# The MLP of a one-layer decoder trunk: sum of squares moved into the up phase, its buffers opened ahead, the first two weight pairs interleaved, the last results of the down product in turn

## The chip, the cores and the metric

The kernel runs on one core of one Trainium2 chip. The metric is device time in microseconds (us) of one execution; the number given for a kernel is the median of its runs. The engines are named as in the profile: PE is TensorE (matmuls; PEld is its weight load), DVE is VectorE, ACT is ScalarE, POOL is GpSimd, SP is SyncE, which here only starts DMAs, in the order of its queue.

## The reference, cut to what matters

One layer, 1024 tokens, model width 1024. After a mixer with three branches and a cross-attention come the parts that matter here:

```
h += CrossAttn(RMSNorm(h), RMSNorm(mem))       # its last step is a product with w_xo
h += W_down( relu(RMSNorm(h) @ W_up)^2 )       # W_up 1024 x 4096, W_down 4096 x 1024

def rms_norm(x, g):
    y = x * rsqrt(mean(x * x) + EPS)
    return y * g
```

Everything is fp32. The kernel holds activations transposed, channels on partitions and tokens along the free dimension: `h` is eight tiles `ht[0]` to `ht[7]` of 128 x 1024. The norm's factor is one number per token, and because `relu(r*x)^2 = r^2 * relu(x)^2` for a positive `r`, it can be left out of the up product and multiplied into the result of the down product. So the sum of squares of `h` over channels is needed only by the end of the down product's first half.

## The kernel before, in words

**Split matmuls.** A fp32 product is made of three matmuls with rounded operands: an operand is split into a rounded high part (a cast on ACT) and the rest (a subtraction on DVE, or on POOL for weights), and high x high, high x low and low x high are added up. In an activation's split the parts are called `oh` and `ol`, in a weight's split `wh` and `wl`; in the up phase one tile holds both: `blk` for activations, `st` for weights.

**The stages at the change.** Three stages follow each other.

1. *The last `w_xo` products* (`project`, L1293 to L1298, and the loop at L1346). Eight products of 24 matmuls each, in the order `ht` 0, 4, 1, 5, 2, 6, 3, 7, from the operands `parts1` (four pairs in pool `opa`). After each, DVE adds the result to `ht` (L1298), SP stores it to the scratch `d_h`, DVE scales it to `v` (L1355), ACT squares it (L1358, L1361) and POOL adds the squares up in `h_acc` (L1362). From the `v` of two tiles (i and i + 4) come the operands of the up phase. That is a Strassen-Winograd product: seven block products take the place of eight, so of each pair of `v` seven blocks are made by `slice_of` (L1331): four quarters or sums of quarters. The names are `x11`, `x21`, `x22` for quarters and `t1` to `t4` for sums of them; `t1` is made at L1367, `t2` at L1371, `t3` at L1375 and `t4` at L1377, all on DVE. `slice_of` casts on ACT (L1336) and subtracts on DVE (L1337). The blocks go into 28 buffers that other work has finished with (`spare`): last among them the tiles `ht` themselves, whose stores must have landed, and pool `opd`.
2. *The up phase* (L1412). Sixteen pairs of `w_up` tiles. For each pair two loads (`ws`: one half in the phase's own pool `up`, one in `wstage`, which the `w_xo` weights use too), three sums on DVE (`s`, L1422 to L1424, and one more at L1429), and seven `stationary` tiles `st`: a cast on ACT (L1407) and a subtraction on POOL (L1408), under high priority. The `st` rotate through ten buffers: six in the pool `wsplit`, which the `w_xo` weights use too, four tagged `oh` in `opa`. Seven products of 12 matmuls follow, in a written order (6, 1, 5, 7, 2, 3, 4; for the first pair 1, 5, 6, 2, 3, 7, 4). Their results go to the four banks `ps_up`, and DVE adds them up (`u`, `r`), squares (L1442) and SP stores them to `d_r`. The bank of product 5 is read until product 7 is done. In the first pair the factor is worked out (`factor`): a column sum by PE, a square root, a diagonal matrix `f_dg` (L260) and its product with ones (`ps_bs`), which spreads the factor over partitions as `rb`.
3. *The down phase* (L1484). Two halves of 512 output channels. Each reads all 32 tiles back from `d_r`, splits each (`split`, ACT L1053 and DVE L1054, four buffers each for `oh` and `ol` in `opb`) and multiplies it with four columns of weights into eight banks: for each tile 24 matmuls. When the 32nd is done, DVE multiplies each bank by `rb` into a tile `o` of two buffers (L1521). In the first half POOL adds `h` (`hv`, read back from `d_h`; L1526) and the whole tile is stored; in the second DVE adds it (L1523) and each half tile is stored.

**What sets the order.** The Tile scheduler orders each engine's instructions by a model of their times, in program order of priority, and each pool's tiles rotate through its buffers. A pool opened after another is closed may lie over its memory; then its tiles wait for what was there. `after(n, f)` calls `f` after n further steps, where a step is called after every few matmuls. The pool `pre`, which holds `v`, `t` and the squares, is closed before the pool `up` opens.

Of the kernel before, what the change touches and what calls it, by code (L numbers as in the profile page):

```python
# [9 lines left out]
F32 = mybir.dt.float32  # L10
# [7 lines left out]
P = 128  # L18
D = 1024
# [36 lines left out]
def trunk_kernel(tc, w_io):  # L56
# [3 lines left out]
    with ctx:  # L60
# [1279 lines left out]
        acc = xr.tile([P, T], F32, tag="acc", name="h_acc3")  # L1340
        with tc.tile_pool(name="pre", bufs=2) as tp:

            rbx = opd.tile([P, T], F32, tag="sl", name="rbx")
            dg = tp.tile([P, T], F32, tag="sq", name="hx_dg", bufs=1)
            after(0, lambda: spread(xr, rx[0], T, "hx", rbx, dg))
            for kp in range(4):  # L1346
                if kp % 2 == 0:
                    slots = [wslot(w_io["w_xo"][1, kp // 2 + 2 * q]) for q in range(2)]
                vs = []
                for q in range(2):  # L1350
                    i = kp + 4 * q
                    project(parts1, slots[q], i // 2, kp % 2)
                    nc.sync.dma_start(d_h[i], ht[i])
                    v = tp.tile([P, T], F32, tag="v", name="v")
                    dve.scalar_tensor_tensor(v, ht[i], C("g_mlp", i), rbx, ALU.mult, ALU.mult)  # L1355
                    vs.append(v)
# [6 lines left out]
                    lo_, hi_ = v[:, :512], v[:, 512:]  # L1363
                    if q == 0:
                        slice_of("x11", lo_)
                        t1 = tp.tile([P, 512], F32, tag="t1", name="t1", bufs=1)
                        dve.tensor_sub(t1, hi_, lo_)  # L1367
                        slice_of("t1", t1)
                t2, t3 = (tp.tile([P, 512], F32, tag="t", name="t") for _ in range(2))
                b12, (b21, b22) = vs[0][:, 512:], (vs[1][:, :512], vs[1][:, 512:])  # L1370
                dve.tensor_sub(t2, b22, t1)  # L1371
                slice_of("t2", t2)
                slice_of("x21", b21)
                slice_of("x22", b22)
                dve.tensor_sub(t3, b22, b12)  # L1375
                slice_of("t3", t3)
                dve.tensor_sub(t2, b21, t2)  # L1377
                slice_of("t4", t2)

        f = []  # L1380

        def factor():

            r = token_rstd(xr, acc, T, 1.0 / D, EPS, "hm")
# [9 lines left out]
        with ExitStack() as sc:  # L1394
            mp = sc.enter_context(tc.tile_pool(name="up", bufs=1))
            after(8, factor)
# [14 lines left out]
            ORDER = (6, 1, 5, 7, 2, 3, 4)  # L1411
            for pr in range(16):  # L1412
                order = ORDER if pr else (1, 5, 6, 2, 3, 7, 4)
                with tc.high_priority():
                    ws = []
                    for q in range(2):
                        w = (wst if q else mp).tile([P, 1024], F32, tag="ws", name="ws", bufs=2)
                        nc.sync.dma_start(w, w_io["w_up"][pr * 2 + q])
                        ws.append(w)
# [21 lines left out]
                def square(o):  # L1441
                    dve.scalar_tensor_tensor(o, o, 0.0, o, ALU.max, ALU.mult)  # L1442
# [192 lines left out]
```

## Time and profile before

| | us |
|---|---|
| median of three runs | 2801.35 |
| lowest and highest | 2796.13, 2801.6 |
| profiled execution | 2799.92 |
| its span, first to last instruction | 2798.1 |

| engine | busy us | share of the span | instructions |
|---|---|---|---|
| PE | 2702.5 | 97% | 12704 |
| PEld | 2181.8 | 78% | 12704 |
| DVE | 1637.3 | 59% | 1858 |
| ACT | 1058.9 | 38% | 1780 |
| POOL | 937.4 | 34% | 460 |

The span runs from the first to the last instruction. All positions in time below are microseconds from its start. The mean granted clock of PE is 0.986 of full speed. The stages of the change lie at the end: the eight `w_xo` products end at 2090.5, the up phase runs from 2113.5 to 2434.7, the down phase from there on.

### The profile page before, as it was taken

How to read it: one execution, taken by the hardware profiler on the slowest of the kernel's cores; microseconds unless marked ns; L12 is line 12 of the kernel's file. 1: busy time of each engine (PE TensorE's matmuls, PEld its weight loads, DVE VectorE, ACT ScalarE, POOL GpSimd, SP SyncE). 2: the span in 40 equal slices, each digit the busy share in tenths (PEclk: the TensorE clock that was granted, in tenths of full speed). 3: DMA queues.
4: the chain of work that ended last, by engine and by line, in shares of the span. 5: the costliest groups of instructions: out<-in, count | busy, mean ns of one | idle time of the engine just before them, and what ended most of it. 6: DMA issues, size and time to landing. Idle time of an engine off the chain costs nothing.

```text
span 2798.1 us, 32362 instructions
## 1 busy us (share of the span) xinstructions
PE 2702.5 (97%) x12704; PEld 2181.8 (78%) x12704; DVE 1637.3 (59%) x1858; ACT 1058.9 (38%) x1780; POOL 937.4 (34%) x460
## 2 busy tenths in 40 slices
PE   8899999999999999999899999999977999999998
PEld 6688878887787878765588778898765888888787
DVE  7678878759777876634414674233386666532322
ACT  6523321213565564556511352245333222233221
POOL 4622222201626252434242522421134554422320
PEclk9999999999999999999999999999997999999999
DMA  6552332321333233542443323311112332454541
GB/s 228 180 144 94 101 115 83 115 105 39 114 113 120 99 127 99 171 140 85 163 162 131 126 93 97 98 54 33 44 68 83 113 113 106 180 188 143 195 131 66
DMA packets 111225, 325.98 MB, mean 117 GB/s; under 512 B 10961, under 2 KB 35937, under 8 KB 110689
## 3 DMA queue, kind: packets, MB, share of 16 engines
q1 hardware_dynamic: 111072, 323.92, 34.4%
q8 instruction: 100, 1.64, 0.2%
q14 instruction: 53, 0.43, 0.1%
HBM read 248.22 MB, written 78.80 MB: 117 GB/s over the span
## 4 chain that ended last, share of the span: by engine, by line
PE 79%; DVE 10%; issue 4%; POOL 2%; DMA 2%; ACT 2%; SPq 0%; DVEq 0%; ACTq 0%; POOLq 0%
PE ps_g L73 34%; PE ps_d L73 12%; PE ps_tm L73 12%; PE ps_up L73 10%; DVE tapy L334 3%; PE ps_yd L73 2%; DVE c4a L744 1%; POOL wl L158 1%; PE ps_lg L73 1%; PE ps_xl L73 1%; PE ps_xo L73 1%; PE ps_pt L77 1%; PE ps_yo L73 1%; PE ps_stt L73 1%; ACT lg L977 1%
## 5 line engine op out<-in xcount | busy, mean ns | idle before, releaser
L158 POOL TENSOR_TENSOR wl<-ws,wh 128x1024 fp32r<-128x1024 f32 x168 | 427.7, 2550 | 1053.2 <-ACT wh L157 993.0
L334 DVE SCALAR_TENSOR_TENSOR tapy<-hin,cst,tapy 128x1024 f32<-128x1024 f32 x240 | 387.7, 1616 | 31.0 <-ACT tapy L329 24.7
L73 PE MATMUL ps_g<-uh,wh 128*128 128x512 f32 x1008 | 330.5, 407 | 12.0 <-ACT uh L353 12.0
L157 ACT CAST wh<-ws 128x1024 fp32r<-128x1024 f32 x168 | 176.2, 1050 | 422.8 <-PE ps_g L73 263.3
L73 PE MATMUL ps_up<-blk,st 128*128 128x512 f32 x1344 | 311.7, 394 | 24.5 <-ACT st L1407 23.0
L73 PE MATMUL ps_g<-ul,wh 128*128 128x512 f32 x1008 | 324.4, 396 | 0.3 <-DVE ul L354 0.3
L73 PEld LDWEIGHTS ps_up<-blk,st 128*128 128x128 f32 x1344 | 255.8, 191 | 80.1 <-ACT st L1407 23.4
L73 PE MATMUL ps_g<-uh,wl 128*128 128x512 f32 x1008 | 315.8, 392 | 1.3 <-POOL wl L158 1.3
L73 PE MATMUL ps_g<-oh,wh 128*128 128x512 f32 x768 | 247.5, 404 | 10.1 <-DVE ht L1298 6.0
L73 PE MATMUL ps_g<-ol,wh 128*128 128x512 f32 x768 | 239.4, 393 | 2.5 <-DVE ol L1054 2.4
L73 PE MATMUL ps_g<-oh,wl 128*128 128x512 f32 x768 | 238.1, 391 | 0.0
L1054 DVE TENSOR_TENSOR ol<-r_in,oh 128x1024 fp32r<-128x1024 f32 x64 | 94.4, 1476 | 234.0 <-ACT oh L1053 231.9
L73 PEld LDWEIGHTS ps_g<-ul,wh 128*128 128x128 f32 x1008 | 190.1, 189 | 50.0 <-issue 9.3
L73 PEld LDWEIGHTS ps_g<-uh,wl 128*128 128x128 f32 x1008 | 189.8, 188 | 43.2 <-POOL wl L158 2.7
L73 PEld LDWEIGHTS ps_g<-uh,wh 128*128 128x128 f32 x1008 | 178.9, 190 | 40.3 <-ACT uh L353 12.0
L73 PE MATMUL ps_d<-oh,wh 128*128 128x512 f32 x512 | 199.9, 390 | 4.4 <-DVE o L1521 4.4
L73 PE MATMUL ps_d<-ol,wh 128*128 128x512 f32 x512 | 199.7, 390 | 0.0
L73 PE MATMUL ps_d<-oh,wl 128*128 128x512 f32 x512 | 199.6, 390 | 0.0
L73 PEld LDWEIGHTS ps_g<-oh,wh 128*128 128x128 f32 x768 | 144.0, 190 | 47.0 <-issue 8.1
L73 PE MATMUL ps_tm<-wh,uh 128*128 128x512 f32 x448 | 175.7, 392 | 0.3 <-DVE zth L590 0.3
L73 PE MATMUL ps_tm<-wh,ul 128*128 128x512 f32 x448 | 174.5, 390 | 0.0
L73 PE MATMUL ps_tm<-wl,uh 128*128 128x512 f32 x448 | 174.3, 389 | 0.0
(380 smaller groups left out, 4676.1 us busy)
## 6 DMA issues: line engine op xcount, KB each, us to landing
ws<-w_ch SPq DMA_DIRECT2D x64, 512.0 KB, 3.4
r_in<-d_r SPq DMA_DIRECT2D x64, 512.0 KB, 3.7
csb<-d_cs SPq DMA_DIRECT2D x32, 512.0 KB, 3.9
gth<-d_th SPq DMA_DIRECT2D x32, 512.0 KB, 4.3
ws<-w_up SPq DMA_DIRECT2D x32, 512.0 KB, 3.2
d_r<-r SPq DMA_DIRECT2D x32, 512.0 KB, 2.6
ws<-w_down SPq DMA_DIRECT2D x32, 512.0 KB, 3.4
d_th<-gate_th SPq DMA_DIRECT2D x21, 512.0 KB, 5.1
```

Of the source, the lines that this page charges most:

```text
L73: ins = nc.tensor.matmul(*a, **k)
L77: ins = nc.tensor.transpose(*a, **k)
L157: act.copy(wh, st)
L158: pool.tensor_sub(wl, st, wh.bitcast(F32))
L334: dve.scalar_tensor_tensor(y, hin[:, j:j + T], w(j), y, ALU.mult, ALU.add)
L744: dve.scalar_tensor_tensor(a[:, s:], v[:, :T - s], C("c4_w", ct * 4 + 3 - s), a[:, s:], ALU.mult, ALU.add)
L977: act.activation(lg[:, i, k0:], lg[:, i, k0:], AF.Exp, bias=nm[:, i:i + 1], accum_out=rs[:, i:i + 1],)
L1054: dve.tensor_sub(b, src, a.bitcast(F32))
```

## The change

- `h`'s squares are no longer made in the first stage. During up pairs 2 to 9, before the first product of each, one tile of `h` is read back from `d_h` into an `ol` buffer of `opa`, squared in place on ACT and added up on POOL. `factor` is called at pair 11, not in the first pair.
- The pool `up` is opened ahead of the `w_xo` loop, and `pre` is gone: `v` and the first diagonal live in `opd`, `t1`, `t2` and `t3` in buffers of `up`. `spare` gives `opd`'s tiles later and the `ht` tiles earlier.
- Pairs 0 and 1 form one group: products 1 and 5 of pair 0, then 1 and 5 of pair 1, then 6, 2, 3, 7, 4 of pair 0 and of pair 1. All fourteen `st` of the group are asked for ahead of its products.
- In the last block of four tiles of a down half, the order is turned: all four tiles are split, and then each of the eight banks gets its remaining 12 matmuls in one go and is taken at once: multiplied, `hv` added on DVE, stored by half tiles, in both halves. `o` uses the eight `ht` buffers.

```diff
-            for pool_, tags, n in ((opc, ("oh", "ol"), 4), (opb, ("oh", "ol"), 4), (opd, ("sl",), 3)):
+            for pool_, tags, n in ((opc, ("oh", "ol"), 4), (opb, ("oh", "ol"), 4), (opd, ("sl",), 1)):
...
-            yield opd, "sl"
+            for _ in range(3):
+                yield opd, "sl"
...
-        acc = xr.tile([P, T], F32, tag="acc", name="h_acc3")
-        with tc.tile_pool(name="pre", bufs=2) as tp:
...
+        with ExitStack() as sc:
+            mp = sc.enter_context(tc.tile_pool(name="up", bufs=1))
...
-            dg = tp.tile([P, T], F32, tag="sq", name="hx_dg", bufs=1)
+            dg = opd.tile([P, T], F32, tag="sl", name="hx_dg")
...
-                    v = tp.tile([P, T], F32, tag="v", name="v")
+                    v = opd.tile([P, T], F32, tag="sl", name="v")
...
-                    if i == 0:
-                        act.activation(acc, ht[i], AF.Square)
-                    else:
-                        sq = tp.tile([P, T], F32, tag="sq", name="sq", bufs=1)
-                        act.activation(sq, ht[i], AF.Square)
-                        pool.tensor_add(acc, acc, sq)
...
-                        t1 = tp.tile([P, 512], F32, tag="t1", name="t1", bufs=1)
+                        t1 = mp.tile([P, 512], F32, tag="p1", name="t1", bufs=2)
...
-                t2, t3 = (tp.tile([P, 512], F32, tag="t", name="t") for _ in range(2))
+                t2 = mp.tile([P, 512], F32, tag="u2", name="t2")
+                t3 = mp.tile([P, 512], F32, tag="u5", name="t3")
...
-            after(8, factor)
...
+            def squares_of(i):
+
+                if i == 0:
+                    sums.append(xr.tile([P, T], F32, tag="acc", name="h_acc3"))
+                hq = opa.tile([P, T], F32, tag="ol", name="h_sq3")
+                nc.sync.dma_start(hq, d_h[i])
+                if i == 0:
+                    act.activation(sums[0], hq, AF.Square)
+                else:
+                    act.activation(hq, hq, AF.Square)
+                    pool.tensor_add(sums[0], sums[0], hq)
...
+            ORDER = (6, 1, 5, 7, 2, 3, 4)
+            groups = [[(0, 1), (0, 5), (1, 1), (1, 5)] + [(pr, j) for pr in range(2) for j in (6, 2, 3, 7, 4)]]
+            groups += [[(pr, j) for j in ORDER] for pr in range(2, 16)]
+            for group in groups:
+                pairs = {}
+                with tc.high_priority():
+                    for pr, j in group:
+                        if pr not in pairs:
+                            pairs[pr] = Pair(pr)
+                        pairs[pr].weights(j)
+                for pr, j in group:
+                    if j == ORDER[0] and 2 <= pr < 10:
+                        squares_of(pr - 2)
+                    elif j == ORDER[0] and pr == 11:
+                        after(0, factor)
+                    pairs[pr].product(j)
...
+                    if blk < 7:
+                        for k in range(4):
+                            operand(blk * 4 + k)
+                            for q in range(4):
+                                for h in range(2):
+                                    product(k, q, h)
+                                step()
+                        continue
+
+                    for k in range(4):
+                        operand(28 + k)
+                    for q in range(4):
+                        i = hf * 4 + q
+                        o = hp.tile([P, T], F32, tag=f"ht{i}", name="o")
+                        for h in range(2):
+                            sl = slice(h * 512, h * 512 + 512)
+                            for k in range(4):
+                                product(k, q, h)
                             step()
...
+                            dve.tensor_mul(o[:, sl], outs[q][h], f[0][:, sl])
+                            dve.tensor_add(o[:, sl], o[:, sl], hs[q][:, sl])
+                            nc.sync.dma_start(w_io["outT"][i][:, sl], o[:, sl])
```

The class `Pair` (new) holds the loads, sums, `st`, products and results of one pair as the loop before did, each made when it is first asked for; `operand(n)` reads tile n of `d_r` and splits it, `product(k, q, h)` is its three matmuls into one bank.

## Rows read from the trace of the kernel before

**Rows 1.** Table by stage: microseconds, busy time (instructions) of five engines, PE's clock, DMA.
```profile
2042.70:2058.50 15.80, 15.80 (x72) 13.07 (x71) 14.74 (x14) 6.63 (x9) 4.58 (x2) 1.00 0.16 66
2058.50:2090.50 32.00, 26.01 (x99) 20.00 (x97) 31.77 (x30) 13.32 (x20) 12.59 (x6) 0.89 0.23 91
2090.50:2113.50 23.00, 0.01 (x2) 0.01 (x1) 19.02 (x20) 7.72 (x13) 8.25 (x4) 0.55 0.22 80
2113.50:2145.00 31.50, 26.38 (x93) 19.59 (x93) 22.85 (x29) 9.97 (x17) 20.83 (x14) 0.77 0.25 84
2145.00:2434.70 289.70, 289.70 (x1274) 239.68 (x1273) 183.94 (x218) 75.23 (x119) 140.03 (x100) 1.00 0.31 114
2611.40:2618.80 7.40, 3.04 (x7) 1.82 (x6) 3.46 (x5) 1.05 (x1) 7.40 (x4) 0.77 0.65 240
2789.10:2798.10 9.00, 0.01 (x1) 0.00 (x0) 5.73 (x10) 0.00 (x0) 0.00 (x0) 0.69 0.49 182
```

**Rows 2.** Waits of PE from 2036 on: total us, times, longest.
```profile
PE ps_up L73 <- ACT st L1407: 23.0, 1, 23.0
PE ps_g L73 <- DVE ht L1298: 6.0, 3, 3.7
PE ps_bs L73 <- DVE f_dg L260: 3.6, 1, 3.6
```

**Rows 3.** Timeline of the SP queue, loads of `w_up`: start, us, instruction.
```profile
2038.68 0.33 SPq L1418 DMA_DIRECT2D ws<-w_up  x1
...
2109.08 23.81 SPq L1418 DMA_DIRECT2D ws<-w_up  x6
...
2257.30 0.33 SPq L1418 DMA_DIRECT2D ws<-w_up  x1
```

**Rows 4.** DVE's groups by form, 2042 to 2109: count, busy us, mean ns, idle before.
```profile
L1371 DVE TENSOR_TENSOR t<-v,t 128x512 f32<-128x512 f32 x4 | 11.0, 2759 | 0.1
L1355 DVE SCALAR_TENSOR_TENSOR v<-ht,cst,rbx 128x1024 f32<-128x1024 f32 x8 | 10.2, 1278 | 0.1
L1298 DVE TENSOR_TENSOR ht<-ht,ps_g 128x1024 f32<-128x1024 f32 x8 | 9.7, 1213 | 6.4 <-PE ps_g L73 6.4
...
L1377 DVE TENSOR_TENSOR t<-v,t 128x512 f32<-128x512 f32 x4 | 7.1, 1767 | 0.0
L1367 DVE TENSOR_TENSOR t<-v 128x512 f32<-128x512 f32 x4 | 6.9, 1723 | 0.1
L1375 DVE TENSOR_TENSOR t<-v 128x512 f32<-128x512 f32 x4 | 2.7, 679 | 0.0
```

**Rows 5.** Timelines of DVE and POOL at 2062: start, us, instruction.
```profile
2062.35 2.77 DVE L1367 TENSOR_TENSOR t<-v 128x512 f32<-128x512 f32 x1
...
2061.75 2.83 POOL L1362 TENSOR_TENSOR h_acc<-h_acc,sq 128x1024 f32<-128x1024 f32 x1 [2.91 <-ACT sq L1361]
```

**Rows 6.** Single lines: count, shortest/median/longest ns, first and last start.
```profile
L1361 ACT ACTIVATE sq<-ht x7: 1050/1062/1066, 2049.5 to 2099.5; 128x1024 f32<-128x1024 f32 x7
...
L1362 POOL TENSOR_TENSOR h_acc<-h_acc,sq x7: 2396/2796/3427, 2050.6 to 2100.6; 128x1024 f32<-128x1024 f32 x7
...
L1408 POOL TENSOR_TENSOR st<-s,st x64: 1262/1286/1807, 2110.5 to 2405.5; 128x512 fp32r<-128x512 f32 x64
```

**Rows 7.** Table by stretch (columns as in rows 1), just after PE's third stop.
```profile
2079.00:2082.00 3.00, 3.00 (x8) 2.32 (x8) 3.00 (x2) 0.62 (x1) 1.41 (x1) 0.50 0.00 0
```

**Rows 8.** Timeline of PE between the halves of down: matmuls ahead of which it stood.
```profile
2615.25 0.79 PE L73 MATMUL ps_d<-oh,wh 128*128 128x512 f32 x1 [3.73 <-DVE o L1521]
...
2618.83 0.50 PE L73 MATMUL ps_d<-oh,wh 128*128 128x512 f32 x1 [0.65 <-DVE o L1521]
```

**Rows 9.** Timelines of PE and DVE at the end.
```profile
2788.72 0.39 PE L73 MATMUL ps_d<-oh,wl 128*128 128x512 f32 x1
...
2785.14 1.29 DVE L1521 TENSOR_TENSOR o<-ps_d,rb 128x512 f32<-128x512 f32 x2 [15.44 <-PE ps_d L73]
...
2793.54 1.29 DVE L1523 TENSOR_TENSOR o<-o,hv 128x512 f32<-128x512 f32 x2
```

More of the change, by code (lines that the diff above doesn't have):

```diff
@@ L1409, in stationary, with __init__ @@
                 return t
[L1411 to L1415, printed above, removed]
+            def squares_of(i):
[8 more added lines that the diff above has]
+                    pool.tensor_add(sums[0], sums[0], hq)
+            sums = []
+            names = {1: "x11", 2: "x21", 3: "x22", 4: "t4", 5: "t1", 6: "t2", 7: "t3"}
+            class Pair:
+                def __init__(self, pr):
+                    self.pr, self.a, self.st, self.banks = pr, [], {}, {}
                     for q in range(2):
@@ L1427, in trunk_kernel @@
-                    for j in order:
-                        if j == 3:
-                            dve.tensor_sub(s2, a12, s2)
-                            st[j] = stationary(s2)
-                        else:
-                            st[j] = stationary(srcs[j])
-                banks = {}
-                names = {1: "x11", 2: "x21", 3: "x22", 4: "t4", 5: "t1", 6: "t2", 7: "t3"}
-                ra, rb_ = (opa.tile([P, T], F32, tag="ol", name="r") for _ in range(2))
-                p1 = mp.tile([P, 512], F32, tag="p1", name="p1", bufs=2)
@@ L1437, in trunk_kernel, with sums @@
[L1437 to L1445 removed]
+                        self.a += [w[:, :512], w[:, 512:]]
+                    self.s = {}
+                def sums(self, n):
+                    if n not in self.s:
+                        a11, a12, a21, a22 = self.a
+                        if n == 2:
+                            self.sums(1)
+                        self.s[n] = t = mp.tile([P, 512], F32, tag="s", name="s", bufs=3)
+                        if n == 1:
+                            dve.tensor_add(t, a21, a22)
+                        elif n == 2:
+                            dve.tensor_sub(t, self.s[1], a11)
+                        else:
+                            dve.tensor_sub(t, a11, a21)
+                    return self.s[n]
@@ new lines, in weights, with product @@
+                def weights(self, j):
+                    a11, a12, a21, a22 = self.a
+                    if j == 3:
+                        s2 = self.sums(2)
+                        dve.tensor_sub(s2, a12, s2)
+                        src = s2
+                    elif j in (1, 2, 4):
+                        src = {1: a11, 2: a12, 4: a22}[j]
+                    else:
+                        src = self.sums({5: 1, 6: 2, 7: 3}[j])
+                    self.st[j] = stationary(src)
+                def product(self, j):
+                    ps = self.banks[j] = pss.tile([P, 512], F32, tag="s", name="ps_up")
+                    st = self.st.pop(j)
@@ L1480, in trunk_kernel @@
             drain()
-        with ExitStack() as sc:
-            dp = sc.enter_context(tc.tile_pool(name="down", bufs=2))
+        if True:
             for hf in range(2):
@@ new lines, in operand, with product @@
+                        ins.append(split(opb, r))
+                    def product(k, q, h):
+                        n = blk * 4 + k
+                        xh, xl = ins[k]
+                        wh, wl = (w[:, k * 256 + q % 2 * P:k * 256 + q % 2 * P + P] for w in slots[q // 2])
+                        sl = slice(h * 512, h * 512 + 512)
+                        pe.matmul(outs[q][h], wh, xh[:, sl], start=n == 0, stop=False)
+                        pe.matmul(outs[q][h], wh, xl[:, sl], start=False, stop=False)
+                        pe.matmul(outs[q][h], wl, xh[:, sl], start=False, stop=n == 31)
```

139 lines of the change are left out of this document (52 added, 87 removed).

## The prediction

> **What bounds the kernel now.** The page's first part comes first: TensorE (PE) is busy 97% of the span, so a change pays only where PE stands still or runs at its lower clock. The table by stage says where [rows 1]. At full clock PE does 1274 matmuls in 289.70 us, 0.2274 us each, and I use that for every matmul below. From 2042.70, where the first of the eight products with `w_xo` is done, to the end of the up phase at 2434.70, PE has 7 x 24 + 1344 = 1512 of them, 343.8 us, and about 2.9 us of small ones for the factor (an estimate: such a group spans 1 to 2 us). The stretch lasted 392.0 us, so it loses 45.3 us, in three places:
>
> - up to 2090.5: 168 matmuls need 38.2 us and took 47.8. Lost: 9.6.
> - the gap: 23.0 us with no work on PE.
> - the up phase, 321.2 us from 2113.5: 305.6 and 2.9 needed. Lost: 12.7.
>
> Two smaller losses are in the down phase: between its halves 7.40 us pass with six or seven matmuls; six need 1.4, so 6.0 are lost. After PE's last matmul 9.0 us pass.
>
> The waits of PE say who ends last [rows 2]: the rounding of the weights (`st`) for the 23.0 us, the addition to `ht` for 6.0, the diagonal `f_dg` for 3.6. In the gap DVE is busy 19.02 of 23.0 us [rows 1], so the name in the wait hides a second cause. `st` came last because the first half of the first weights was not loaded before 2109.08, when six loads go out in a row, while a second half was asked for at 2038.68 [rows 3]; and DVE had finished its last block only just before.
>
> Why is DVE late? In its rows for the stretch [rows 4] operations of one shape have two durations: `t3` (L1375) takes 679 ns, `t2` (L1371) 2759, `t1` 1723 and `t4` 1767 on average. The excess is 4 x (2.08 + 1.04 + 1.09) = 16.8 us. One `t1` that lasts 2.77 us starts at 2062.35, inside an addition of squares on GpSimd that runs from 2061.75 to 2064.58 [rows 5]: it ends 0.54 us after it, about its own length. I call this a collision. There were seven such additions of 2.4 to 3.4 us [rows 6].
>
> The Trainium skill's page SBUF — State Buffer (section Who interferes with whom) says that a DVE operation with two SBUF inputs and a GpSimd operation reading SBUF exclude each other for a whole instruction. The pair of rows agrees. The rule speaks against this change as well as for it, since the subtractions of the weights that move forward read SBUF on GpSimd too; the second rival below is its case.
>
> **The change part by part.** *Sum of squares out of the first stage.* It takes eight Squares of 1.06 us off ACT and seven additions off GpSimd here [rows 6]. Each addition cost DVE up to 2.1 us, so some 14 of the 16.8 us go. DVE's list for two products is then 2 x 1.21 + 2 x 1.28 + 10 x 0.68 = 11.8 us by durations, about 11.0 by starts (one begins as the one before drains), against 10.9 for PE's 48 matmuls. The two become equal. Of the three stalls for `ht` (6.0 us) and the low clock after the longest (granted 0.50 [rows 7], some 3 us lost) nearly all goes. I take 8.6 of 9.6; bounds 3 (half the lag stays) and 9.6.
>
> *Buffers opened ahead.* The first weights land about 2045 instead of 2113. The added early work: two sums on DVE (1.4 us), and as many `st` as have buffers. `st` rotates through ten: six in the pool that the `w_xo` weights use, four in the one that holds `parts1` until the last product. So two can be made early, two after the last product but one, the rest only as PE finishes. By DVE's list: it restarts at 2048.2; the rest of the first two products 7.4, the next four 22, then addition, `v`, `x11`, `t1` and their blocks 4.3: 2081.9. Add the sums 1.4, a collision with the one `wl` left (2.1, as with an addition) and with about three `st` subtractions of 1.28 [rows 6] (I take 1.0 each, 3.0): 2088.4, and the last block of `x11` 0.6 before. PE ends its `w_xo` products at 2081 to 2082 and can do nine of the twelve matmuls of the first up product; so it stands from about 2084 to 2087.5, 3.5 us, and then loses 2.5 to 3 at the low clock as after its stop of 3.74 us. The gap shrinks from 23 to 6: gain 17. Bounds: 8 (all fourteen subtractions of the group come before the blocks: 14 x 0.9, and the low clock) and 23.
>
> *First two pairs interleaved.* Four products come first that need only `x11` and `t1`: 10.9 us of PE work. Beside them runs the chain of the last `ht`: 1.21, 1.28, 0.68 (`t2`), ACT's 0.62, 0.68, about 4.5 us, and four collisions. It ends near 2097, when PE gets to the last quarter of the first product with `t2`. After that a block is needed every 2.7 us and made in 0.68 to 1.75. Two of the four `ps_up` banks are now held (product 5 of both pairs) until product 7, so each product waits for the drain of the one two before it, 0.7 to 1.8 us against 2.7. Block `x21` takes the place of the last `ht`, whose store must land first (about 5 us); it is needed 13 us later. Cost of all three: 0, behind PE's queue; without that cover, 0.5 to 2 us a product for ten products, the low end of the next part's bounds.
>
> *Up phase.* Its loss of 12.7 is 5.1 us of waits (the 0.65 and 0.83 behind the gap and the 3.64 for `f_dg`) and a granted clock of 0.77 over its first 31.5 us [rows 1], about 7. The factor moves to pair 11, into the stretch where DVE is busy 183.94 of 289.70 us. I leave 3.0 (the wait for `f_dg` may stay): gain 9.7, bounds -3 and 12.7. Eight reloads of 512 KB, eight Squares and seven additions come in: ACT is busy 75 and GpSimd 140 of 290 us there, so their 9 and 18 us are hidden, with weights made up to ten products ahead. If that cover went, 18 us on GpSimd would be the price.
>
> *Down.* Between the halves PE waited on DVE, 3.73 and 0.65 us [rows 8], and DVE (by the code) on a store of `o` to free one of two buffers. Now `o` has eight (dead `ht`), GpSimd's four additions go, and each result is drained while the next 12 matmuls (2.7 us) run; DVE's eight more additions of 0.69 are hidden there. New: all four operands stay until the last result, so the next half's first operand is split only after its buffer's last reader, 2.0 us before the end; ACT's 1.06 and DVE's 1.23 make it about 0.5 late, with a collision up to 2. I leave 1.0 of 6.0: gain 5.0, bounds 3 and 6.
>
> At the end [rows 9], DVE takes the first result at 2785.14 and works until 2794.83, though PE ended at 2789.11. Now only one multiplication and addition follow: 2789.11 + 0.1 + 1.29 = 2790.5. Gain 4.3, with the same store behind it; bounds 3.5 and 4.5.
>
> **Sum.** 8.6 + 17 + 9.7 + 5.0 + 4.3 = 44.6 us off the profiled execution's 2799.92 us (span 2798.1): 2755.3. The median of the runs is 2801.35, the lowest 2796.13; 1.4 us don't matter here. I predict 2755.
>
> **The rivals.**
> *Everything is covered.* All of 45.3 + 6.0 + 4.3 = 55.6 goes: 2744. For it: the lists of PE and DVE are equal. Against: then nothing is left for collisions.
> *DVE stays the bound through collisions.* The moved subtractions and sums (14 x 0.9 and 8 x 0.68 = 18 us) take back what the squares released. First stage 4, gap 9, up 5, down 9.3: 27 us, 2773. For: the weights have priority. Against: only two to four have a buffer in time.
> *The buffers open no earlier.* If the up pool lies over memory that something holds until the blocks are done, the gap stays. The first stage's 8.6, up 4, down 9.3: 22, 2778. Against: its pool now opens before the first of these `w_xo` products.
> *Slower.* The SP queue works in order. A reload of `d_h` waits for one of four `ol` buffers, and the `w_up` loads behind it wait too. Those go out about a pair (19 us) ahead, as at 2257.30 [rows 3]; a transfer takes about 3.3, so the first 15 us of such a wait cost nothing, and each one more costs PE eight times. From 21 us a reload the gain is gone; at 22, 56 us are lost: 2811. Against: two results and a reload fit in four buffers.
>
> **Chances.** Forecast (2748 to 2764) 0.60; all covered 0.13; collisions 0.14; buffers no earlier 0.06; slower 0.04; partial failures that end within 0.2% 0.03. About 0.2% (5.6 us) is what a measurement of this kernel can tell from no change. Faster 0.93, same 0.03, slower 0.04. The range takes in the first three cases, 2743 to 2775, and leaves out mainly the others.
>
> **What would show it.** Right: no addition of squares on GpSimd among the `w_xo` products and `t2` near 0.7 us; the first `w_up` loads of both halves before 2050; PE's stop before the first `ps_up` under 7 us; an up phase of 308 to 313 us; no wait of PE for `o` between the halves; DVE's last operation about 1.4 us after PE's last. Wrong: slow `t` beside `st` subtractions, a gap over 12 us, or SP waiting for `ol` ahead of a `w_up` load.

## The result, and the profile after

| | us | ratio to the kernel before (95% interval) |
|---|---|---|
| before, median of four runs | 2799.98 | |
| after, median of four runs | 2767.01 (2765.97 to 2769.85) | 0.9886 (0.9869 to 0.9903) |
| predicted | 2755 (2743 to 2775) | |

The kernel is 33 us faster where 45 were forecast. The profiled execution took 2765.97 us (span 2763.9) at a mean granted clock of 0.994; it is compared here with the profiled 2799.92 us (span 2798.1) before.

Positions ahead of the change differ by a few microseconds between executions: the first `v` on DVE starts at 2044.1 before and at 2040.5 after, and between 2040.4 and 2045.8 in all the traces of this study, though that work is unchanged. So all lengths are counted from that start. The up phase runs from the first matmul into `ps_up`, the down phase from the first to the last into `ps_d`; the tail is what follows it.

| us | first `v` to up | up | down | tail | first `v` to end |
|---|---|---|---|---|---|
| before | 69.4 | 321.1 | 354.2 | 9.4 | 754.0 |
| after | 39.3 | 321.9 | 357.3 | 4.8 | 723.4 |

The gain is 30.6 us from that start; the other 3.6 of the two spans' difference lie ahead of it. All of the gain comes before the first up product and in the tail. The up phase got no shorter, the down phase 3.2 us longer.

The table by stretch after the change: microseconds, busy time (instructions) of PE, PEld, DVE, ACT and POOL, PE's clock, DMA share, GB/s.
```profile
2039.10:2055.00 15.90, 15.90 (x72) 13.17 (x71) 14.88 (x18) 5.22 (x8) 2.97 (x1) 1.00 0.18 69
2055.00:2079.90 24.90, 22.43 (x100) 18.24 (x99) 23.18 (x28) 9.15 (x16) 6.95 (x4) 1.00 0.34 125
2079.90:2110.00 30.10, 21.73 (x76) 16.38 (x75) 26.31 (x31) 12.86 (x23) 16.91 (x11) 0.83 0.27 88
2110.00:2401.80 291.80, 291.61 (x1292) 240.75 (x1291) 207.81 (x235) 85.52 (x130) 159.56 (x108) 1.00 0.37 131
2555.90:2583.00 27.10, 23.30 (x91) 17.68 (x90) 13.87 (x17) 3.92 (x5) 4.52 (x2) 0.94 0.59 202
```
Against [rows 1] the gap of 23.0 us has gone, and the second row loses 2.5 of its 24.9 us where the first stage lost 9.6. But the third row has only 76 matmuls in 30.1 us. At 0.2274 us each they need 17.3, so 12.8 are lost: what the up phase lost before, at the same place, now for another reason. From 2110 to the end of the up phase PE stands 0.2 us in all. The waits of PE name that reason (total us, times, longest):
```profile
PE ps_up L73 <- DVE blk L1338: 5.7, 2, 4.3
PE ps_d L73 <- DVE o L1568: 3.1, 4, 0.8
PE ps_up L73 <- ACT blk L1337: 2.7, 2, 2.0
PE ps_g L73 <- DVE ht L1298: 2.5, 1, 2.5
PE ps_d L73 <- DVE ol L1054: 2.1, 1, 2.1
PE ps_bs L73 <- DVE f_dg L260: 0.2, 1, 0.2
```
No weight is waited for any more. `f_dg` fell from 3.6 to 0.2, `ht` from three stops to one [rows 2]. New are the blocks of the last pair of `v`, and two waits in the down phase. The stop for `ht` that is left has its own cause, a weight sum ahead of that addition on DVE's list:
```profile
2057.89 0.75 DVE L1438 TENSOR_TENSOR s<-ws 128x512 f32<-128x512 f32 x1 [1.62 <-DMA ws<-w_up]
```
DVE stood 1.62 us there for a load that went out only at 2053.82, the second half of pair 1. Two more sums follow before the addition starts, at 2062.06. In the run without these sums (no_sums, below) the stop is 0.2 us.

**At the head of up.** PE's timeline there: start, us, instruction, in brackets how long it stood before it and what released it.
```profile
2084.01 0.50 PE L73 MATMUL ps_up<-blk,st 128*128 128x512 f32 x1 [1.95 <-ACT blk L1337]
2088.86 4.95 PE L73 MATMUL ps_up<-blk,st 128*128 128x512 f32 x11 [4.34 <-DVE blk L1338]
2094.56 0.49 PE L73 MATMUL ps_up<-blk,st 128*128 128x512 f32 x1 [0.75 <-ACT blk L1337]
2096.37 33.88 PE L73 MATMUL ps_up<-blk,st 128*128 128x512 f32 x141 [1.32 <-DVE blk L1338]
```
These are 8.4 us of stops, and the rest of the 12.8 is the lower clock (0.83 granted in that row, 1.00 in the next). The timeline of DVE in that stretch:
```profile
2081.75 1.27 DVE L1370 SCALAR_TENSOR_TENSOR v<-ht,cst,rbx 128x1024 f32<-128x1024 f32 x1
2084.19 1.74 DVE L1449 TENSOR_TENSOR s<-ws,s 128x512 f32<-128x512 f32 x1 [1.17 <-POOL st L1401]
2085.85 1.28 DVE L1338 TENSOR_TENSOR blk<-t,blk 128x512 fp32r<-128x512 f32 x2
2087.05 1.75 DVE L1338 TENSOR_TENSOR blk<-v,blk 128x512 fp32r<-128x512 f32 x1
2088.72 1.75 DVE L1440 TENSOR_TENSOR s<-s,ws 128x512 f32<-128x512 f32 x1
2090.40 1.77 DVE L1442 TENSOR_TENSOR s<-ws 128x512 f32<-128x512 f32 x1
2092.09 1.76 DVE L1376 TENSOR_TENSOR t<-v 128x512 f32<-128x512 f32 x1
2093.78 1.21 DVE L1298 TENSOR_TENSOR ht<-ht,ps_g 128x1024 f32<-128x1024 f32 x1
2095.02 0.69 DVE L1449 TENSOR_TENSOR s<-ws,s 128x512 f32<-128x512 f32 x1
```
And of POOL:
```profile
2084.11 1.26 POOL L1401 TENSOR_TENSOR st<-ws,st 128x512 fp32r<-128x512 f32 x1
...
2086.66 3.28 POOL L1401 TENSOR_TENSOR st<-s,st 128x512 fp32r<-128x512 f32 x2 [1.28 <-ACT st L1400]
2089.89 3.41 POOL L1401 TENSOR_TENSOR st<-ws,st 128x512 fp32r<-128x512 f32 x2
```
Read the two lists side by side. DVE's block of `x11` (2087.05) ends at 2088.80, and PE goes on at 2088.86. Ahead of it stands a weight sum (L1449) that first waits 1.17 us for POOL and then lasts 1.74 us; the same operation at 2095.02, with no subtraction beside it, lasts 0.69. The block itself lasts 1.75. Then come two more sums and a `t`, each 1.75 beside a subtraction, all ahead of the last addition to `ht`: that starts at 2093.78, although PE had finished its matmuls at 2079.8. So DVE finishes its last block 67.2 us after the first `v`; before it was 64.8.

The squares did leave the first stage. DVE's groups from 2038 to 2108 (count, busy us, mean ns, idle before), the answer to [rows 4]:
```profile
L1376 DVE TENSOR_TENSOR t<-v 128x512 f32<-128x512 f32 x4 | 3.8, 958 | 0.1
...
L1381 DVE TENSOR_TENSOR t<-v,t 128x512 f32<-128x512 f32 x4 | 2.8, 688 | 0.1
L1387 DVE TENSOR_TENSOR t<-v,t 128x512 f32<-128x512 f32 x4 | 2.7, 684 | 0.0
L1385 DVE TENSOR_TENSOR t<-v 128x512 f32<-128x512 f32 x4 | 2.7, 683 | 0.0
```
The operations on `t` that took 2759, 1767 and 1723 ns now take 688, 684 and 958. Their place in the up phase costs PE nothing: the seven additions on POOL (2394 to 2514 ns) run from 2150.2 to 2264.5, where PE never stands.

**In down.** PE, then DVE and POOL, at the end of its first half:
```profile
2558.78 0.50 PE L73 MATMUL ps_d<-ol,wh 128*128 128x512 f32 x1 [2.09 <-DVE ol L1054]
2560.29 0.50 PE L73 MATMUL ps_d<-oh,wh 128*128 128x512 f32 x1 [0.78 <-DVE o L1568]
```
```profile
2556.17 2.56 DVE L1054 TENSOR_TENSOR ol<-r_in,oh 128x1024 fp32r<-128x1024 f32 x1 [4.98 <-ACT oh L1053]
2559.55 0.69 DVE L1568 TENSOR_TENSOR o<-ps_d,rb 128x512 f32<-128x512 f32 x1 [0.83 <-PE ps_d L73]
```
```profile
2555.26 2.38 POOL L158 TENSOR_TENSOR wl<-ws,wh 128x1024 fp32r<-128x1024 f32 x1 [0.32 <-ACT wh L157]
```
The split of tile 31, which used to have 24 matmuls to hide behind, now meets a weight's subtraction on POOL and takes 2.56 us instead of 1.23. (At the end of the second half, at 2736.28, POOL does nothing; the split takes 1.23 us and PE stands 0.14 for it.) The second stop is that of the first matmul into the *second* half of a result: it waits until DVE has read the *first*. There are four of these, 0.78 us each, two in each half of down (2560.29, 2568.45; 2739.07, 2745.59). The first two of the four results lie in tiles of 128 x 1024, a pair of halves in one tile, the last two in tiles of their own, and those have no stop.

At the end, DVE's last two operations, to be held against [rows 9]:
```profile
2759.55 0.69 DVE L1568 TENSOR_TENSOR o<-ps_d,rb 128x512 f32<-128x512 f32 x1 [1.30 <-PE ps_d L73]
2760.27 0.69 DVE L1569 TENSOR_TENSOR o<-o,hv 128x512 f32<-128x512 f32 x1
```
PE's last matmul starts at 2759.12; 4.8 us follow, 9.4 before.

### The profile page after: what moved, and what is told of

Read it like the earlier page. It is cut to its first block, busy times and chain, and to the rows that moved or that the text cites. A ratio compares the mean times of both kernels' runs of the same rounds, so it can differ in the third digit from the quotient of the medians.

```text
span 2763.9 us, 32384 instructions
## 1 busy us (share of the span) xinstructions
PE 2696.0 (98%) x12704; PEld 2178.0 (79%) x12704; DVE 1645.7 (60%) x1866; ACT 1056.7 (38%) x1780; POOL 929.6 (34%) x456
```

## The experiments

The kernel before had medians of 2798.3, 2799.34, 2798.73 and 2798.68 us in the four groups of runs. Medians and ratios are against the one of the same group; the columns in us are from the traces, counted as above.

| run | median | ratio (95%) | to up | up | down | tail | to end |
|---|---|---|---|---|---|---|---|
| down_only | 2796.63 | 0.9994 (0.9985 to 1.0004) | 69.4 | 321.2 | 355.7 | 4.8 | 751.1 |
| down_before | 2772.99 | 0.9909 (0.9894 to 0.9924) | 41.1 | 321.9 | 354.2 | 9.7 | 726.8 |
| banks | 2762.72 | 0.9868 (0.9852 to 0.9885) | 39.4 | 321.8 | 353.0 | 4.8 | 719.0 |
| banks_k3 | 2760.02 | 0.9864 (0.9850 to 0.9879) | 39.4 | 321.8 | 349.7 | 4.8 | 715.8 |
| squares_only | 2775.21 | 0.9913 (0.9898 to 0.9928) | 53.6 | 312.8 | 355.9 | 9.4 | 731.6 |
| squares_back | 2783.40 | 0.9949 (0.9933 to 0.9966) | 47.2 | 328.1 | 357.3 | 5.1 | 737.6 |
| one_pair | 2769.52 | 0.9895 (0.9880 to 0.9910) | 38.3 | 324.5 | 358.5 | 4.8 | 726.2 |
| late_weights | 2768.57 | 0.9890 (0.9873 to 0.9906) | 38.5 | 323.9 | 357.0 | 4.8 | 724.2 |
| no_sub | 2762.60 | 0.9870 (0.9855 to 0.9885) | 38.2 | 318.3 | 358.5 | 4.8 | 719.7 |
| no_sums | 2761.85 | 0.9868 (0.9853 to 0.9883) | 37.1 | 319.5 | 355.7 | 4.8 | 717.2 |
| dve_sub | 2769.27 | 0.9893 (0.9876 to 0.9909) | 39.4 | 320.4 | 358.3 | 4.8 | 722.9 |
| k_last | 2762.18 | 0.9869 (0.9855 to 0.9884) | 38.8 | 323.0 | 349.7 | 4.8 | 716.3 |

One code's down phase differs by 2 to 3 us between executions (354.2 before and 355.9 in squares_only; 355.7 to 358.5 in the eight kernels with the down phase of after), so columns are compared to no better than that. The difference lies at the end of the first half, where the last 96 matmuls take 26.2 to 29.1 us in those eight with the same stops; at the end of the second half they take 24.1 in each of the eight.

### The down part alone, and all but it

The first is the kernel before with the down phase of after, of which the core is this; the second is the kernel after with this edit undone.
```diff
+                    for q in range(4):
+                        i = hf * 4 + q
+                        o = hp.tile([P, T], F32, tag=f"ht{i}", name="o")
+                        for h in range(2):
+                            sl = slice(h * 512, h * 512 + 512)
+                            for k in range(4):
+                                product(k, q, h)
```

> The kernel before with the new down phase alone. First theory: the new order of the last block takes away the stop between the halves (6.0 us) and most of the tail (4.3), but puts four stops of 0.78 us in their place, where a matmul into the second half of a two-bank tile waits until DVE has read the first half, and a stop of 2.1 us at the fourth operand with a low clock behind it: net gain 1 to 2 us, 2798 to 2799. Rival: the down part is worth the 9 us of the prediction and the up phase lost the rest: 2791.

> The changed kernel with the down phase of before. First theory: 1 to 2 us slower than the changed kernel (2768 to 2769), with the stop between the halves (4.4 us and a low clock) and the long tail back. Rival: 9 us slower (2776).

Alone, the down part moves nothing that can be measured: 4.6 us come off the tail and 1.5 go back into the down phase by the trace, with the same four stops for `o` (3.1 us) and one for `ol` (2.1). The first theory holds. The second gave 2772.99, between the two expectations; its trace is 3.4 us longer than after's, half of it ahead of the up phase, where the two programs ask for the same work. The medians are 6 us apart. The two profiled executions are 6.9 apart, and the other half of that lies ahead of the change: the first `v` starts at 2044.0 here and at 2040.5 in after. Whether the medians differ for that reason stays open, so this run settles neither expectation.

### The order of the eight results

```diff
-                    for q in range(4):
...
-                        for h in range(2):
+                    for q, h in ((0, 0), (1, 0), (0, 1), (1, 1), (2, 0), (2, 1), (3, 0), (3, 1)):
```


> The changed kernel; in the last block of a down half the banks are taken in the order q0 h0, q1 h0, q0 h1, q1 h1, then q2 and q3 as they were, so that no product follows directly the other half of its own two-bank tile. First theory (the two halves of a tile count as one for the wait): the four stops of 0.78 us go, 3.5 to 4 us gained, 2763. Rival (the stop is DVE being late with its work, wherever the bank lies): the stops stay, 2767.

The two halves of one tile are no longer neighbours, so a whole result's 12 matmuls lie between them. PE's stops in the last blocks of down, of which one is left:
```profile
2561.45 0.50 PE L73 MATMUL ps_d<-ol,wh 128*128 128x512 f32 x1 [2.09 <-DVE ol L1054]
```
All four stops of 0.78 went, and the down phase is 4.3 us shorter. 2.1 us of it are at the end of the second half, where the last 96 matmuls take 22.0 instead of 24.1; the other 2.2 are at the end of the first, no more than that varies by. The theory holds.

### Tile 31 later

To the version above, the first three of the four tiles' matmuls of two results are put ahead, so that tile 31 is needed nine matmuls later.
```diff
+                        if (q, h) == (0, 0):
+                            for q2 in range(2):
+                                for k in range(3):
+                                    product(k, q2, 0)
+                        for k in range(3 if h == 0 and q < 2 else 0, 4):
```


> As e_banks, and of the first two banks the matmuls with the fourth operand come only after those with the first three operands of both (18 matmuls, 4.1 us, before the fourth operand is needed instead of 9, 2.0 us). First theory: the stop of 2.1 us and the low clock behind it (1.7 us) in the first half go as well, 2759 to 2760. Rival: the operand is late by the rotation of its buffer and the stop only moves: as e_banks.

The same view as above:
```profile
2560.47 0.50 PE L73 MATMUL ps_d<-ol,wh 128*128 128x512 f32 x1 [0.22 <-DVE ol L1054]
```
The stop of 2.09 fell to 0.22, the down phase by another 3.2 us, and it is as long in k_last (349.7 us), which has the same down phase. Down and tail together are now 354.5 us against 363.5 before. With 2760.02 us this is the fastest version of this study. By medians its lead over the one before is inside both spreads (2758.64 to 2764.42 there, 2758.98 to 2762.19 here); the traces show it.

### The squares alone, and all but the squares

The first is the kernel before with the squares and the factor moved into the up phase, and nothing else. Its edit:
```diff
-                    if i == 0:
-                        act.activation(acc, ht[i], AF.Square)
...
-            after(8, factor)
...
+                if 2 <= pr < 10:
+                    squares_of(pr - 2)
+                elif pr == 11:
+                    after(0, factor)
                 for j in order:
```
The second is the kernel after with the squares back beside the `w_xo` products (in halves, for want of a buffer); the factor stays at pair 11:
```diff
+                        for h in range(2):
+                            sl = slice(h * 512, h * 512 + 512)
+                            sq = mp.tile([P, 512], F32, tag="p1", name="sq", bufs=2)
+                            act.activation(sq, ht[i][:, sl], AF.Square)
+                            pool.tensor_add(sums[0][:, sl], sums[0][:, sl], sq)
...
-                    if j == ORDER[0] and 2 <= pr < 10:
-                        squares_of(pr - 2)
```

> The kernel before with only the sum of squares moved: its additions on GpSimd and Squares on ACT leave the first stage, the reloads come in pairs 2 to 9, the factor in pair 11; the up pool opens after the blocks as before. First theory (the excess of DVE's operations is the collision with these additions): t2 falls to 0.7 us, DVE ends its blocks about 14 us earlier, the three stops for ht go, the gap before the up phase stays above 15 us because the weights still start after the blocks; 12 to 17 us faster than before, 2783 to 2788. Rival (DVE's slow operations come from something else): within 3 us of before.

> The changed kernel with the sum of squares back in the first stage (in two halves each, in the buffers of the up pool that t1 uses: 14 additions of 512 columns on GpSimd instead of 7 of 1024); buffers ahead, interleaving, factor in pair 11 and the new down phase stay. Theory (DVE's list with its collisions is the bound of the stretch, and the moved squares are worth most of the gain): the collisions and the early sums and subtractions add up, the blocks end some 10 to 14 us later than in the changed kernel, and PE loses as much: 2776 to 2784. Rival (the buffers opened ahead carry the gain, as the prediction weighted it with 17 of 45 us, and the squares only 9 to 10): 2772 to 2776, with stops for ht as before and no more than 5 us of new stops in the up phase.

The squares alone gave 2775.21, some 8 us better than forecast. The operations on `t` take 685 to 691 ns, all three stops for `ht` are gone, and the gap shrinks without a buffer being opened earlier:
```profile
2095.54 1.22 PE L73 MATMUL ps_up<-blk,st 128*128 128x512 f32 x2 [16.87 <-ACT st L1413]
```
Before it were 23.0 us, since the pool could only open when DVE was through its list: 49.3 us after the first `v` here, 64.8 before. In both the next loads of `w_up` go out within 0.2 us of that (2091.30 here, 2109.08 before). The up phase loses 8.3 us less; how much of that is the factor's later place (its wait fell from 3.6 to 0.2) and how much a DVE with no backlog was not separated.

The second gave 2783.40, inside the first theory's 2776 to 2784: with the squares back, the stops for `ht` return. PE's waits:
```profile
PE ps_g L73 <- DVE ht L1298: 7.7, 3, 5.4
PE ps_up L73 <- ACT blk L1337: 6.6, 2, 6.0
PE ps_up L73 <- DVE blk L1338: 5.4, 2, 4.3
```
Up to the end of the up phase the squares alone gain 24 us, everything else alone 15, both together 29. The parts overlap by 10. Some 3.4 us of that are the factor's: it stands at pair 11 in both of these kernels, so its wait is gained in both. The rest is put down, without a run of its own, to DVE's list, into which the buffers opened ahead bring a part of the next phase's work: its last block ends at 49.3 us with the squares alone moved and at 67.2 in after.

### One pair first

```diff
-            groups = [[(0, 1), (0, 5), (1, 1), (1, 5)] + [(pr, j) for pr in range(2) for j in (6, 2, 3, 7, 4)]]
-            groups += [[(pr, j) for j in ORDER] for pr in range(2, 16)]
+            groups = [[(0, j) for j in (1, 5, 6, 2, 3, 7, 4)]]
+            groups += [[(pr, j) for j in ORDER] for pr in range(1, 16)]
```


> The changed kernel without the interleaving: pair 0 alone in the order 1, 5, 6, 2, 3, 7, 4 of before, then pair 1. First theory: only two products (5.4 us) stand between the last w_xo product and the first product with t2, whose chain ends later, so PE stops once more for 3 to 6 us: 2770 to 2774. Rival (interleaving only pulls pair 1's sums and subtractions ahead of the last blocks on DVE): faster than the changed kernel by 2 to 5 us.

By the trace it is 2.8 us longer than after, 1.2 of it in the down phase, whose code is the same; by the medians the two can't be told apart. It is not faster, as the rival had it, nor did the theory's stop of 3 to 6 us come. PE's timeline shows three of its four stops, for the last blocks of `x11`, `t1` and `t2`:
```profile
2091.91 0.79 PE L73 MATMUL ps_up<-blk,st 128*128 128x512 f32 x1 [6.63 <-ACT blk L1337]
...
2101.68 4.36 PE L73 MATMUL ps_up<-blk,st 128*128 128x512 f32 x12 [3.43 <-DVE blk L1338]
2106.51 23.87 PE L73 MATMUL ps_up<-blk,st 128*128 128x512 f32 x104 [0.46 <-DVE blk L1338]
```
The first two stand where after stands too. Only at `t2`, 0.46 us, does the interleaved order have other products to do, so no worth of the interleaving could be measured.

### The weights of the first group asked for later

```diff
-                        pairs[pr].weights(j)
-                for pr, j in group:
+                        if pr > 1 or j in (1, 5):
+                            pairs[pr].weights(j)
+                for n, (pr, j) in enumerate(group):
+                    if pr < 2 and n + 4 < len(group):
+                        pairs[group[n + 4][0]].weights(group[n + 4][1])
```


> The changed kernel; of the first group only the four weights that the first four products need are made under high priority, each later one is asked for four products ahead of its product with normal priority, behind the last blocks. First theory (the stops of 8.4 us in the first products, with the low clock some 12.8 us, come from sums and subtractions that stand ahead of the last blocks on DVE): the stops before x11 and t1 of the last pair fall below 4 us in all, 6 to 10 us gained, 2757 to 2761. Rival (DVE's own list is too long, in whatever order): the same loss, 2765 to 2769, or the weights themselves come late and it is slower.

If only the order of DVE's list were wrong, this would have mended it. One stop of 5.40 us takes the place of the first two of after (1.95 and 4.34), but it is followed by others later, and the end is 0.8 us later than after's:
```profile
2108.73 2.98 PE L73 MATMUL ps_up<-blk,st 128*128 128x512 f32 x12 [1.55 <-ACT st L1400]
2114.69 2.96 PE L73 MATMUL ps_up<-blk,st 128*128 128x512 f32 x12 [2.97 <-DVE r L1489]
```
The sums put off now stand ahead of DVE's draining of results. DVE's last block ends 56.8 us after the first `v`, ten earlier than in after, but the one that PE waits for first, the last of `x11`, only 1.1 earlier (47.1 against 48.2). The theory that this order is at fault falls. That the list is too long in any order fits, and is shown for this order alone.

### Work taken off the list

Three kernels lighten it in different ways. The first leaves out the low parts of the first fourteen `st` (ACT copies the source in their place), the second the sums of the first two pairs, the third moves the fourteen subtractions from POOL to DVE.
```diff
-                pool.tensor_sub(t[:, 1, :], src, t[:, 0, :].bitcast(F32))
+                if nstat[0] <= 14:
+                    act.copy(t[:, 1, :], src)
+                else:
+                    pool.tensor_sub(t[:, 1, :], src, t[:, 0, :].bitcast(F32))
```


> The changed kernel with the low part of the fourteen weights of the first group left out: GpSimd's subtraction is replaced by a cast on ACT (0.62 us), so nothing on GpSimd reads beside DVE there; the low parts are wrong. Theory (collisions of DVE with these subtractions, about eleven at 1.07 us, are what makes the last blocks late): the stops of 8.4 us and the low clock fall to a third, 7 to 10 us gained, 2757 to 2760. Rival (the sums of the weights on DVE alone): at most 3 us, 2764.


```diff
+                    if self.pr < 2:
+                        return self.a[n]
...
-                        dve.tensor_sub(s2, a12, s2)
+                        if self.pr > 1:
+                            dve.tensor_sub(s2, a12, s2)
```


> The changed kernel without the eight sums of the first two pairs on DVE (the weights are taken as they are, so the products of these pairs are wrong); the subtractions on GpSimd stay. Theory (collisions): 2 to 4 us gained, since eight operations of 0.6 us and their places ahead of the blocks go but the collisions stay, 2763 to 2765. Rival (the sums ahead of the blocks, with what they wait for, are the cause): 8 to 10 us, 2757 to 2759.


```diff
-                pool.tensor_sub(t[:, 1, :], src, t[:, 0, :].bitcast(F32))
+                low = dve if nstat[0] <= 14 else pool
+                low.tensor_sub(t[:, 1, :], src, t[:, 0, :].bitcast(F32))
```


> The changed kernel with the subtractions of the fourteen weights of the first group on DVE (0.68 us each) instead of GpSimd (1.28). Theory (collisions): fourteen times 0.6 on DVE replaces about eleven collisions of 1.07 and the waits of DVE's sums for GpSimd: 1 to 4 us gained, 2763 to 2766. Rival (DVE's list is the bound and collisions are cheap): 5 to 8 us slower, 2772 to 2775.

To the start of the down phase, leaving out the subtractions is worth 4.8 us and leaving out the sums 4.6: both between the two expectations, the sums nearer to the theory's. Moving the subtractions changes nothing that can be told (1.4 us to there, 0.4 to the end), and its 2769.27 too lies between theory and rival. The busy table of the 84.5 us from the first `v`, in the order after, no_sub, no_sums, dve_sub (columns as above):
```profile
2040.50:2125.00 84.50, 73.66 (x304) 59.05 (x303) 75.61 (x88) 30.66 (x52) 34.85 (x22) 0.94 0.29 100
```
```profile
2040.40:2124.90 84.50, 77.19 (x325) 62.27 (x324) 71.66 (x93) 38.78 (x68) 14.25 (x10) 0.94 0.30 109
```
```profile
2043.90:2128.40 84.50, 76.25 (x325) 61.87 (x324) 76.00 (x85) 31.40 (x54) 36.81 (x24) 0.94 0.30 107
```
```profile
2045.80:2130.30 84.50, 73.25 (x311) 59.48 (x310) 77.90 (x103) 30.99 (x53) 12.01 (x8) 0.94 0.28 101
```
The last against the first: POOL is relieved of 23 us, DVE does fifteen operations more in this stretch, and is busy only 2.3 us longer (77.90 against 75.61). Here a subtraction beside its list costs DVE nearly as much as one in it. A stop for a block of the last pair remains in each: 5.94 us in no_sub, 4.41 and 3.63 in no_sums, 8.30 in dve_sub. In no_sums and dve_sub ACT casts the last of `x11` within 0.1 us of the end of its `v`, so the wait named after ACT is DVE's. In no_sub it is ACT's: `v` is done at 2081.23, and the cast comes 4.8 us later, behind eight casts of `st`, of which four are the copies that this kernel makes in place of subtractions:
```profile
2086.03 0.61 ACT L1337 CAST blk<-v 128x512 fp32r<-128x512 f32 x1
```
DVE itself ends its last block 55.9 us after the first `v` there, against 67.2 in after and 59.8 in no_sums. So 4.8 us is the least that the subtractions cost PE.

### More of PE's work put ahead of the late block

To banks_k3, three quarters of each of the first four products are done first, the two that need `x11` ahead of the two that need `t1`.
```diff
+            FIRST = [(0, 1), (1, 1), (0, 5), (1, 5)]
...
+                    for ks in ((0, 1, 2), (3,)):
+                        for pr, j in FIRST:
+                            pairs[pr].product(j, ks)
```


> e_banks_k3, and of the first four up products first the matmuls with the first three blocks of each (36, 8.2 us), then those with the fourth, x11 ahead of t1. If only the order of use makes PE stop, the stops at x11 and t1 (8.4 us) fall below 3 and 5 to 8 us are gained on e_banks_k3 (2752 to 2755). If DVE's whole list is the bound (blocks, sums, drains, collisions), the wait moves to the next products: 0 to 3 us gained, 2757 to 2760.

PE can do 36 matmuls, 8.2 us, before it needs a block of the last pair. It stood all the same:
```profile
2092.51 0.50 PE L73 MATMUL ps_up<-blk,st 128*128 128x512 f32 x1 [1.72 <-ACT blk L1337]
2097.75 2.93 PE L73 MATMUL ps_up<-blk,st 128*128 128x512 f32 x6 [4.73 <-DVE blk L1338]
```
With other stops of 0.67, 1.25 and 0.19 it ends 0.6 us later than banks_k3, and its 2762.18 lies above both expectations. Where PE has other work, the stop only moves: DVE ends its last block 68.5 us after the first `v`, 67.9 in banks_k3.

## Why the prediction came out as it did

The time lies inside the range and above the likeliest case's 2748 to 2764. Its terms against the traces, from the first `v`:

| part | predicted gain | measured |
|---|---|---|
| first stage, gap and up phase | 8.6 + 17 + 9.7 = 35.3 | 29.2 |
| between the halves of down, and end | 5.0 + 4.3 = 9.3 | 1.4 |
| sum | 44.6 | 30.6 |

- **First stage.** One stop of 2.47 us for `ht` is left of the 9.6 us: a gain of 7.1 for the 8.6 taken. Collisions with the squares were the cause: without them `t2` takes 0.69 us. The sign named in the prediction was there. The stop that is left comes from the early sums and the load that one of them waits for; the prediction counted the sums in the gap alone.
- **Gap and up.** The first loads went out at 2030.65, and three had landed by 2038.4, for the forecast 2045. Only the second half of pair 1 came late (out at 2053.82, where 2050 was the sign). The stop that was to come before the first up product came inside it, after nine matmuls, and so is counted in the up phase, which took 321.9 us where 308 to 313 were the sign of being right. Gap and up phase together lost 35.7 us and now lose about 13: a gain of 22.7 for the 26.7 taken. The mechanism was the forecast one, a wait for the last blocks; its size was off. 6.0 us were put down for its stop and low clock, with 3.0 more left in the up phase; 12.8 were lost at one place. The step allowed two early sums at full speed (1.4 us) and three collisions of 1.0. The list shows three sums of 1.75 and one wait of 1.17 between the last but one addition to `ht` and the last, and blocks and `t` of 1.75 as well. From the first `v` to that last addition seven operations of DVE lie beside subtractions of `st` and last some 1.07 us longer each, 7.5 us for the 3.0 put down. Four `st` were made before PE ended its `w_xo` products, as the step had it, but seven more followed at once and came ahead of that addition. Taking out the subtractions gave at least 4.8 us back and taking out the sums 4.6, so the second rival's mechanism was at work, at about half of its 18 us, if the two add up, which no run shows.
- **The weights of the parts.** The prediction gave the buffers and what goes with them more than the squares. The pair of runs says the reverse, 15 against 24 us (the factor's place in both), and that the two don't add up. The 17 us for the gap were worked out on a DVE list without the squares, so they were never a price of the buffers alone; that the sum for the three stages came as near as 6 us says little for its parts.
- **Factor and reloads.** Of the 3.0 us left for `f_dg`, 0.19 came. The reloads and additions were costed at nothing, and so it was: PE never waits for `h_acc`.
- **Down: the step that failed.** "Each result is drained while the next 12 matmuls (2.7 us) run" overlooked that for two of the eight results of each half of down the next 12 matmuls go into the other half of the same tile, and wait for the drain. [Rows 9] could have warned: counted back from PE's last matmul by 0.2274 us each, the first half of the first result was done at 2784.3 and the second at 2785.0, and DVE began only at 2785.14, after both. And of the split of tile 31, "0.5 late, with a collision up to 2": the collision came, 2.09 us, and the lower clock behind it. So between the halves 6.0 us of losses became about 6.5 and not 1.0. At the end the tail gained 4.6 and the last 96 matmuls, with the two stops, took 2.6 back (24.1 against 21.5). Both errors are shown by the runs: with the order of results changed and tile 31 put off, down and tail gain 9.0 us, for the 9.3 predicted.
- **The rivals.** "Everything is covered" fell with the 12.8 us. The buffers did open earlier. The reloads held up no load of `w_up`: SP stood 0.2 us in all ahead of them, and PE 0.2 us in all from 2110 to the end of the up phase.

## What to carry to other kernels

When work is taken off one engine's list and other work is opened ahead of time beside it, write that engine's list as it will stand, operation by operation, with the longer duration for each that meets an operation it collides with; here the list ended no earlier than before. Before counting a drain as hidden, see in which tile the next matmuls land: halves of one tile may wait for each other, and changing the order of two loops was worth 4.3 us. Undo each part alone and do each part alone: gains that free the same engine don't add up.

## What the runs showed of the hardware

- **Collisions work both ways, in turns.** Two-input operations of DVE beside subtractions of POOL take 1.75 us instead of 0.69, and POOL's take 3.28 and 3.41 for two instead of 1.26 for one; four of DVE's in a row start 1.68 us apart. One of each per 1.68 us, where both alone would take 0.69 + 1.26 = 1.95 one after the other: nearly nothing is gained by running them side by side. That dve_sub took 23 us of busy time off POOL and gave DVE only 2.3 more is the same thing seen from the other end. The Trainium skill's page SBUF — State Buffer (Who interferes with whom) states that two such operations exclude each other; the trace agrees to within the 0.27 us by which 1.68 is less than 1.95.
- **A wait by tile.** Four stops of 0.78 us stood where PE wrote one half (128 x 512) of a 128 x 1024 tile while DVE read the other, and none where the halves were tiles of their own. That is how this program's waits are set; whether the chip would need them was not tried.
- **Small stops cost more than they last.** At the end of the second half of down, two stops of 0.78 us are 1.6 us in the waits. The last 96 matmuls take 24.1 us there in all eight traces with these stops and 22.0 in banks without them, 2.1 less, at a granted clock of 1.00 in both. The first matmul behind such a stop lasts 0.50 us, those after it 0.39 to 0.40.
